# Gathering tokens for 32 experts with one fp32 copy and an unsplit fp32 bias in place of three bf16 parts

## The chip, the cores and the metric

The kernel runs on one core of a Trainium2 chip. The metric is device time in microseconds (us): the median of several executions. TensorE is called PE in the rows, and its weight loads PEld; DVE is VectorE, ACT is ScalarE, POOL is GpSimd, SP is SyncE, whose queue issues the loads of weights.

## What is computed

Two transformer blocks of two and one layers on 256 tokens of width 1024, all in fp32. The first block (an RG-LRU mixer, a forgetting attention, two squared-ReLU MLPs) and the hybrid mixer of the second block (stick-breaking attention beside an HGRN2 recurrence) are not touched by the change. What follows them is:

```python
h = layer_norm(ALPHA * h + mix, ln1_g, ln1_b)
ffn = moe(h, router_w, router_b, w_up, b_up, w_down, b_down)
h = layer_norm(ALPHA * h + ffn, ln2_g, ln2_b)

def moe(h, ...):
    logits = xt @ router_w + router_b            # 256 x 32
    top_vals, top_idx = lax.top_k(logits, 4)
    gates = jax.nn.softmax(top_vals, axis=-1)
    ...
    hcat = xblk @ w_up[e] + b_up[e]              # 1024 -> 2048
    x_glu = jnp.minimum(hcat[:, 0::2], 7.0)
    x_lin = jnp.clip(hcat[:, 1::2], -7.0, 7.0)
    act = x_glu * jax.nn.sigmoid(1.702 * x_glu) * (x_lin + 1.0)
    return act @ w_down[e] + b_down[e]           # 1024 -> 1024
```

Each of the 32 experts computes the block for the tokens that chose it, and each token sums its four experts' rows by its gates.

## The kernel before

*Dense part.* Up to about 830 us the kernel runs the two mixers, the MLPs and the projections. A weight arrives as a raw fp32 block of 1 MiB, `[128, 2048]`, is split into a rounded high part and a low rest (`split_to`, L370: ScalarE casts, VectorE or GpSimd subtracts), and `three` (L468) multiplies with three matmuls. The raw blocks rotate over a pool `rawA` of `NA = 5`, and `load_ahead` (L347) issues them on SP's queue.

*Experts.* After the router, `expert(pos)` (L1984) runs 32 times, in an order that `rank_experts` finds from the counts: position 0 and 1 hold experts 0 and 1, whose weights are known beforehand, and the rest are sorted. A unit is 64 slots for tokens. Every position has one unit, but position 12 has two (`WIDE`), so there are 33 units. For each, in this order on PE:

- `first_bias` (L1542): four matmuls that spread the expert's row of `b_up` over the 64 slots. `bup3` holds the 32 rows of `b_up` three times, as three bf16 parts, on 96 partitions; the weights are a 0/1 column of `Qb` that picks the three rows.
- `first_layer` (L1745): 8 chunks of `w_up`, each 1 MiB, four fp32 matmuls of 512 columns to a chunk, with the 64 gathered tokens as weights. Both halves of the output lie in two banks, a lower and an upper 64 partitions each. In the middle of it `combine` (L1835) adds the previous unit to the tokens.
- `turned_gates` (L1735): the tile `pG`, two transposes that give the slots' gates and the one-hot `PT`.
- `gather_units(pos + 1)` with `gather` (L1714): the next unit's tokens. The normed x is held in three bf16 parts `n3` whose sum is the fp32 value. For each of three parts, two token halves and eight feature blocks, one matmul has the part as weights (128 x 128) and the one-hot `P` (128 x 64) as moving operand: 48 matmuls into one bank `pX`. VectorE takes it out into `xT` with the norm's gain and bias.
- `turned` (L1790): the tile `paT`, the gated activation `xl` turned; and `second_layer` (L1801): four chunks of `w_down`.

While the first layer's results pass `gated` (L1758) on VectorE and ScalarE, PE does `pG` and the gather, which stand between the first layer and `paT` in its order.

```python
for i, t in ((0, 0), (1, 0), (0, 1), (1, 1), (2, 0), (2, 1)):
    for k in range(KT):
        pe.matmul(p[:, k], n3p[:, i, t, k // 2, k % 2], P[:, t],
```

*The order around it.* All order is that of the code. Small jobs that belong to expert 0 and 3 (ranking, `residual_sum`, `list_overflow`) are hung on chunks by the table `later` (L1974). The expert weights go through 20 chunk slots, 20 MiB. Some are filled by `fill` (L315) while the dense part still runs, as its pools close, and then `release` (L1987) calls `load_to`, which loads chunk n+20 when chunk n is used. A slot pool in `paired` holds two chunks that one DMA of 2 MiB loads; 12 of the 20 slots are such pairs. The other eight take 1 MiB each.

*Between router and experts.* The turned x for the router lies in `turned_x`, in one of the slots (`rawE`). The normed x is made in three parts by `high` (ScalarE, L1614) and `rest` (GpSimd for one token half, VectorE and ScalarE for the other, L1616 to L1632), interleaved with `best` and `chosen`, the routing. The bias parts are made earlier: `bias_parts` (L1459, VectorE casts) and `bias_rest` (L1463, GpSimd subtracts), hung among the last projections, whose weight splits (L368, L390) use the same engines. Before expert 0, PE also runs `pg`, eight transposes that spread the norm's gain over the tokens (L1682), for `residual_sum` (L1895).

Of the kernel before, what the change touches and what calls it, by code (L numbers as in the profile page):

```python
# [20 lines left out]
D = 1024  # L21
# [10 lines left out]
NA, NF, NG, NB = 5, 4, 2, 1  # L32
# [45 lines left out]
def shape_constants():  # L78
# [12 lines left out]
    f["ranks"] = np.broadcast_to(rank_of_position(), (128, NE))  # L91
# [6 lines left out]
    f["first"] = (i[:, None] % NE == np.arange(2)) & (i[:, None] < 3 * NE)  # L98
# [23 lines left out]
def fused(ctx: ExitStack, tc: tile.TileContext, d, out, dbg=None):  # L122
# [11 lines left out]
    rawA = ctx.enter_context(tc.tile_pool(name="rawA", bufs=NA, side="right"))  # L134

    def raw_tile():
        return rawA.tile([128, 2048], F32, tag="raw", name="raw")
# [209 lines left out]
    def load_ahead(n):  # L347
        while state["loaded"] < min(n, len(plan), *[i + NA for i in whole[:1]]):
            i = state["loaded"]
            r = raw_tile()  # L350
# [13 lines left out]
    def low_parts(left):  # L364

        while len(lows) > left:
            e, wl, src, wh = lows.pop(0)
            e.tensor_sub(wl, src, wh)  # L368

    def split_to(h):  # L370

        while state["split"] <= min(h, 2 * len(plan) - 1):
# [12 lines left out]
            for q in (slice(0, 512), slice(512, 1024)) if i == 0 else (slice(0, 1024),):  # L385
                copy, sub = [e[n % len(e)] for e in state["share"]]
                if copy == "d":
                    dve.tensor_copy(wh[:, q], src[:, q])
                else:
                    act.copy(wh[:, q], src[:, q])  # L390
                lows.append((pool if sub == "p" else dve, wl[:, q], src[:, q], wh[:, q].bitcast(F32)))
            low_parts(1 if state["late"] else 0)
            k, c = plan[i][1], 2048 // plan[i][1]
# [785 lines left out]
    with ExitStack() as mixo, ExitStack() as attn:  # L1179
# [239 lines left out]
        fill((4, second), (6, rawA), (7, rawA))  # L1419
# [5 lines left out]
        third = ctx.enter_context(tc.tile_pool(name="third", bufs=1, side="right", reuse_waits="tile"))  # L1425
        fill((10, third))
# [18 lines left out]
        rawB = ctx.enter_context(tc.tile_pool(name="rawB", bufs=NB, side="right", reuse_waits="tile"))  # L1445
        bup = rawB.tile([128, 2048], F32, tag="raw", name="bup")
        for g in range(3):
            sp.dma_start(bup[32 * g:32 * g + 32], d["expert_b_up_2"][0])
# [4 lines left out]
        mb = ctx.enter_context(tc.tile_pool(name="bias", bufs=1, side="right", reuse_waits="tile"))  # L1453
        bup3 = mb.tile([128, 2 * D], BF, name="bup3")
        pool.memset(bup3[96:128], 0.0)

        def bias_parts(n):

            dve.tensor_copy(bup3[:n], bup[:n])  # L1459

        def bias_rest(n):
            for c in (0, 1024):
# [4 lines left out]
        branch(1, 1, "w_branch_hgrn_2", [lambda: (bias_parts(96), bias_rest(64))])  # L1467
# [5 lines left out]
        first_b = mo.tile([128, 2], BF, name="first_b")  # L1473
# [4 lines left out]
        pool.tensor_copy(first_b, C("first"))  # L1478
# [35 lines left out]
        def out_proj(w, steps, first=False, hooks={}):  # L1514
            for i, k in steps:
# [4 lines left out]
                for f in hooks.get(i, ()):  # L1520
                    f()

        out_proj(w, [(i, i) for i in range(4)], True, {1: [lambda: bias_parts(64), lambda: bias_rest(32)]})
        w = row_weights(d["w_out_2"][0], 512, 512)
        out_proj(w, [(0, 4), (1, 5)], False, {0: [lambda: bias_parts(32)]})
# [24 lines left out]
        xs = [turned_x[:, t].rearrange("p (k t) -> p k t", k=KT) for t in range(2)]  # L1550
        n3 = mo.tile([128, 3, 2, D], BF, name="n3")
# [56 lines left out]
        def halves(t, c):  # L1608
            return x[:, t, c * 512:(c + 1) * 512], parts_of[:, t, c * 512:(c + 1) * 512], \
                [n3[:, i, t, c * 512:(c + 1) * 512] for i in range(3)]  # L1610

        def high(t, c):
            xx, rr, nn = halves(t, c)
            act.activation(nn[0], xx, AF.Identity, scale=rn[t], bias=nm[t])  # L1614

        def rest(t, c):  # L1616

            xx, rr, nn = halves(t, c)
            if t == 0:
                pool.tensor_scalar(rr, xx, rn[t], nm[t], op0=OP.mult, op1=OP.add)  # L1620
                yield
                pool.tensor_sub(rr, rr, nn[0])
                act.copy(nn[1], rr)
                yield
                pool.tensor_sub(nn[2], rr, nn[1])
            else:
                dve.scalar_tensor_tensor(rr, xx, rn[t], nn[0], op0=OP.mult, op1=OP.subtract)
                yield
                act.activation(nn[1], rr, AF.Identity, bias=nm[t])
                yield  # L1630
                dve.scalar_tensor_tensor(nn[2], rr, nm[t], nn[1], op0=OP.add, op1=OP.subtract)
            yield  # L1632

# [527 lines left out]
```

## Time and profile before

| what | value |
|---|---|
| median of 3 runs | 1775.71 us (1775.11 to 1777.3) |
| the profiled execution, its time | 1776.4 us |
| the profiled execution, its span | 1774.6 us |
| mean granted clock of TensorE | 0.983 |
| busy share: PE, PEld, DVE, ACT, POOL | 94%, 63%, 52%, 29%, 5% |
| mean DMA rate over the span, bytes moved | 303 GB/s, 538.55 MB |
| first layer of expert 0 begins | 839.11 us |
| last expert begins | 1725.88 us |

The span runs from the first to the last instruction; the execution's time is 1.8 us longer. A busy share is an average over a dense part and an expert part, which have different limits. In the timeline, adjacent instructions of one line are one row: "x32" counts the matmul records, of which an fp32 matmul has two, and the time of a row reaches to the end of the last, while the next row may begin before, since matmuls are pipelined. The time from start to start is what a group of them costs. A granted clock of 1.00 is 2.4 GHz, the lower level is 1.2 GHz.

### The profile page before, as it was taken

The numbers are of one execution on the slowest core, as the hardware profiler recorded it, in microseconds if no ns is written. First come the engines' busy times: TensorE is split into PE (matmuls) and PEld (weight loads), VectorE is DVE, ScalarE is ACT, GpSimd is POOL, SyncE is SP. The second block draws the span as 40 slices with busy tenths as digits, with TensorE's granted clock in tenths as the row PEclk, the third lists the DMA queues.
The fourth block names the chain that finished last, engine by engine and source line by source line (L and its number), as shares of the span: only waits on it lengthen the run. The fifth ranks groups of instructions, "written<-read, shape, count | busy, mean of one in ns | idle before, by whom it ended". The sixth has DMA issues, their size and how long they took to land.

```text
span 1774.6 us, 28179 instructions
## 1 busy us (share of the span) xinstructions
PE 1665.0 (94%) x11633; PEld 1112.0 (63%) x11633; DVE 928.4 (52%) x1681; ACT 514.4 (29%) x793; POOL 91.1 (5%) x102
## 2 busy tenths in 40 slices
PE   8999999989999999999998999999999988898895
PEld 8899998988999999997333333343333333333331
DVE  7776668677665667777435334334334333333233
ACT  5654444545444455544110010101010110101011
POOL 4020000001000001125000000000000000000000
PEclk9999999999999999999999999999999999999998
DMA  8465554333555544477999999999999999999995
GB/s 276 145 220 186 190 181 140 109 124 126 180 188 190 173 161 143 169 285 277 406 425 423 425 424 422 425 424 423 422 424 424 424 425 422 425 423 424 423 424 217
DMA packets 102532, 538.55 MB, mean 303 GB/s; under 512 B 7985, under 2 KB 21457, under 8 KB 68001
## 3 DMA queue, kind: packets, MB, share of 16 engines
q1 hardware_dynamic: 101520, 534.69, 76.7%
q0 software_dynamic: 736, 1.95, 0.4%
q8 instruction: 93, 1.52, 0.4%
q14 instruction: 39, 0.31, 0.0%
q10 hardware_dynamic: 144, 0.07, 0.0%
HBM read 535.64 MB, written 1.05 MB: 302 GB/s over the span
## 4 chain that ended last, share of the span: by engine, by line
PE 61%; DMA 21%; DVE 10%; ACT 4%; issue 2%; POOL 1%; SPq 0%; ACTq 0%; DVEq 0%; POOLq 0%
DMA raw<-in_expert_w_up_dram 21%; PE hp L1754 15%; PE py L1818 8%; PE pf L471 5%; PE pf L469 5%; PE pf L470 5%; PE a L470 4%; PE a L471 4%; PE a L469 4%; DVE wl L368 2%; PE a L826 1%; PE pC L1840 1%; DVE xl L1778 1%; DVE sgm L1775 1%; PE paT L1796 1%
## 5 line engine op out<-in xcount | busy, mean ns | idle before, releaser
L1754 PE MATMUL hp<-raw,xT 128*64 128x512 f32 x2112 | 479.1, 605 | 25.3 <-DMA raw<-in_expert_w_up_dram 24.5
L368 DVE TENSOR_TENSOR wl<-raw,wh 128x1024 fp32r<-128x1024 f32 (+1 forms) x235 | 288.2, 1244 | 140.8 <-ACT wh L390 138.7
L1754 PEld LDWEIGHTS hp<-raw,xT 128*64 128x64 f32 x2112 | 150.4, 139 | 316.7 <-issue 264.5
L390 ACT CAST wh<-raw 128x1024 fp32r<-128x1024 f32 (+1 forms) x238 | 242.1, 1039 | 170.4 <-PE pf L470 94.5
L471 PE MATMUL pf<-hH,wl 128*128 128x256 f32 x928 | 259.8, 280 | 7.4 <-DVE wl L368 7.4
L469 PE MATMUL pf<-hH,wh 128*128 128x256 f32 x928 | 261.9, 282 | 1.1 <-ACT wh L390 1.0
L470 PE MATMUL pf<-hL,wh 128*128 128x256 f32 x928 | 258.9, 279 | 0.0
L1818 PE MATMUL py<-raw,aT 128*64 128x512 f32 x1056 | 236.0, 599 | 17.4 <-ACT aT L1798 16.4
L471 PEld LDWEIGHTS pf<-hH,wl 128*128 128x128 f32 x928 | 174.3, 188 | 9.3 <-DVE wl L368 9.3
L469 PEld LDWEIGHTS pf<-hH,wh 128*128 128x128 f32 x928 | 174.3, 188 | 1.8 <-ACT wh L390 1.5
L1831 DVE SCALAR_TENSOR_TENSOR y<-py,gcol,y 64x512 fp32r<-64x512 f32 x66 | 49.5, 751 | 238.1 <-ACT y L1830 238.0
L470 PEld LDWEIGHTS pf<-hL,wh 128*128 128x128 f32 x928 | 174.0, 187 | 0.1
L1818 PEld LDWEIGHTS py<-raw,aT 128*64 128x64 f32 x1056 | 73.1, 137 | 158.0 <-issue 131.2
L1841 DVE TENSOR_TENSOR x<-x,pC 128x512 f32<-128x512 f32 x128 | 79.4, 682 | 176.6 <-PE pC L1840 176.6
L1769 ACT ACTIVATE sgm<-sgm 128x256 f32<-128x256 f32 x66 | 27.5, 417 | 492.2 <-DVE sgm L1768 492.2
L471 PE MATMUL a<-aH,wl 128*128 128x256 f32 x512 | 145.0, 283 | 0.0
L469 PE MATMUL a<-aH,wh 128*128 128x256 f32 x512 | 144.9, 283 | 0.0
L470 PE MATMUL a<-aL,wh 128*128 128x256 f32 x512 | 144.9, 283 | 0.0
L1830 ACT ACTIVATE y<-py,gcol 64x512 fp32r<-64x512 f32 x66 | 45.1, 683 | 261.2 <-issue 219.9
L1768 DVE TENSOR_SCALAR sgm<-hp 128x256 f32<-128x256 f32 x66 | 27.7, 419 | 145.0 <-PE hp L1754 145.0
L469 PEld LDWEIGHTS a<-aH,wh 128*128 128x128 f32 x512 | 98.3, 192 | 0.0
L471 PEld LDWEIGHTS a<-aH,wl 128*128 128x128 f32 x512 | 98.2, 192 | 0.0
(494 smaller groups left out, 2082.7 us busy)
## 6 DMA issues: line engine op xcount, KB each, us to landing
raw<-in_expert_w_up_dram SPq DMA_DIRECT2D x77, 2048.0 KB, 24.8
raw<-in_expert_w_up_dram SPq DMA_DIRECT2D x102, 1024.0 KB, 24.7
raw<-in_expert_w_down_dram SPq DMA_DIRECT2D x38, 2048.0 KB, 24.8
raw<-in_mlp_w_dram SPq DMA_DIRECT2D x64, 1024.0 KB, 5.4
raw<-in_expert_w_down_dram SPq DMA_DIRECT2D x51, 1024.0 KB, 24.8
raw<-in_w_in_dram SPq DMA_DIRECT2D x22, 1024.0 KB, 5.2
raw<-in_fox_w_in_dram SPq DMA_DIRECT2D x12, 1024.0 KB, 5.4
raw<-in_lru_w_in_dram SPq DMA_DIRECT2D x6, 1024.0 KB, 12.9
```

The lines of the kernel that those rows point to most:

```text
L368: e.tensor_sub(wl, src, wh)
L390: act.copy(wh[:, q], src[:, q])
L469: pe.matmul(out_ap, lh, rh, start=first, stop=False, skip_group_check=True)
L470: pe.matmul(out_ap, lh, rl, start=False, stop=False, skip_group_check=True)
L471: pe.matmul(out_ap, ll, rh, start=False, stop=last, skip_group_check=True)
L1754: pe.matmul(hp[b][64 * g:64 * g + 64], xT[:, k], w[:, c0:c0 + 512], start=False, stop=(k == KT - 1), skip_group_check=True)
L1768: dve.tensor_scalar_min(sgm[b], hv[b][:, :, 0], 7.0)
L1769: act.activation(sgm[b], sgm[b], AF.Sigmoid, scale=1.702)
L1818: pe.matmul(py[c], aT[:, j, g * 64:(g + 1) * 64], w[:, i * D + c * 512:i * D + c * 512 + 512], start=(kt == 0), stop=(kt == KT - 1), skip_ ...
L1830: act.activation(y[0:64, s], py[c], AF.Copy, scale=gcol[h])
L1831: dve.scalar_tensor_tensor(y[64:128, s], py[c], gcol[h], y[0:64, s].bitcast(F32), op0=OP.mult, op1=OP.subtract)
L1841: dve.tensor_add(x[:, t, s], x[:, t, s], p)
```

## The change

1. The normed x becomes one fp32 tile `nx` that four ScalarE operations write. The turned x for the router lies in the same tile before. `high`, `rest`, `parts_of` and `n3` are gone, and GpSimd's part in them.
2. `gather` has 16 fp32 matmuls (eight blocks, two token halves) in place of 48 in bf16; `P` is fp32. In expert 0 it writes three banks in turn, otherwise one, taken out by two VectorE operations of 128x512 in place of four of 128x256.
3. `bup` holds the bias unsplit: each quarter of 512 columns on 32 partitions of its own. `Q` has four blocks of 0/1 columns, and `first_bias` four fp32 matmuls. `bias_parts` and `bias_rest` are gone.
4. `rawA` is one tile `area`, of which parts serve as raw blocks and as slots. 18 of 20 slots are in pairs. The last four dense loads rotate over three blocks of it. Slot pair 18 takes the place that `turned_x` had, at the closing of `wp2x`, and the third pair of slots (10) is filled later, after the attention's pools close.
5. In expert 0, `residual_sum` and its `pg` matmuls are at chunk 5, `by_position` at chunk 4, and the bias of expert 1 at chunk 7. Some memsets are smaller or gone.

```diff
-        for g in range(3):
-            sp.dma_start(bup[32 * g:32 * g + 32], d["expert_b_up_2"][0])
+        bup = mb.tile([128, 512], F32, name="bup")
+        for g in range(4):
+            sp.dma_start(bup[32 * g:32 * g + 32], d["expert_b_up_2"][0][:, g * 512:(g + 1) * 512])
...
-            dve.tensor_copy(bup3[:n], bup[:n])
...
-                pool.tensor_sub(bup[:n, c:c + 1024], bup[:n, c:c + 1024], bup3[:n, c:c + 1024])
...
+            k = (i - TAKEN) % NA if i < TAKEN else 2 + (i - TAKEN) % 3
+            r = area[:, k * 2048:(k + 1) * 2048]
...
-        fill((4, second), (6, rawA), (7, rawA))
+        fill((4, second), (6, parts_A[0]))
...
-        turned_x = rawE.tile([128, 4, D], F32, tag="raw", name="turned_x")
+        fill((18, rawE))
...
-        fill((11, rawA), (12, rawA), (13, rawA))
+        fill((12, parts_A[1]), (16, parts_A[2]))
...
         def first_bias(hps, sel):
...
-                        c0 = g * D + b * 512
-                        pe.matmul(hp[b][64 * g:64 * g + 64], sel.to_broadcast([128, SLOTS]),
-                                  bup3[:, c0:c0 + 512], start=True, stop=False, skip_group_check=True)
+                        pe.matmul(hp[b][64 * g:64 * g + 64], sel[:, 2 * g + b].to_broadcast([128, SLOTS]), bup,
+                                  start=True, stop=False, skip_group_check=True)
...
-        n3 = mo.tile([128, 3, 2, D], BF, name="n3")
+        nx = mo.tile([128, 2, D], F32, name="nx")
+        xs = [nx[:, t].rearrange("p (k t) -> p k t", k=KT) for t in range(2)]
...
-        for t, c in ((1, 0), (0, 0), (1, 1), (0, 1)):
-            high(t, c)
+        for t in range(2):
+            for c in range(2):
+                h = slice(c * 512, (c + 1) * 512)
+                act.activation(nx[:, t, h], x[:, t, h], AF.Identity, scale=rn[t], bias=nm[t])
...
-        for i, t in ((0, 0), (1, 0), (0, 1), (1, 1), (2, 0), (2, 1)):
-            for k in range(KT):
-                pe.matmul(p[:, k], n3p[:, i, t, k // 2, k % 2], P[:, t],
-                          start=(i + k + t == 0), stop=(i == 2 and t == 1), skip_group_check=True)
+        for s in (slice(0, 2), slice(2, 5), slice(5, 8)) if quick else (slice(0, KT),):
+            p = mm("pX").rearrange("p (k s) -> p k s", k=KT)
+            for k in range(s.start, s.stop):
+                for t in range(2):
+                    pe.matmul(p[:, k], nxp[:, t, k // 2, k % 2], P[:, t], start=(k == s.start and t == 0),
+                              stop=(k == s.stop - 1 and t == 1), skip_group_check=True)
...
-        dve.tensor_scalar(Q, C("ranks"), rk, None, op0=OP.is_equal)
-        dve.tensor_copy(Qb, Q)
+        dve.scalar_tensor_tensor(rk4, rk.to_broadcast([128, 4]), 1.0, C("block"), op0=OP.add, op1=OP.mult)
+        dve.tensor_tensor(Q, C("ranks")[:, None, :].to_broadcast([128, 4, NE]),
+                          rk4[:, :, None].to_broadcast([128, 4, NE]), op=OP.is_equal)
...
-        (0, 1): [lambda: residual_sum(1), gates_of_tokens],
+        (0, 1): [gates_of_tokens],
...
-        (0, 5): [by_position],
+        (0, 4): [by_position],
+        (0, 5): [residual_sum],
+        (0, 7): [lambda: first_bias(early_hps[1], first_b[:, :, 1:2])],
```

The order of instructions on PE around the start of the experts, before. `cd`, `pl` are the router's operands, `route_b` the constants that count tokens before each one; of rows that repeat a pattern the first stand here:

```order
L1581 MATMUL pl<-cd,turned_x 128x32 x8
L1547 LDWEIGHTS first_b
L1547 MATMUL hp<-bup_8541,first_b 64x512
...
L1682 MATMUL pg<-ident,V 128x128 x8
L1685 LDWEIGHTS route_b
L1685 MATMUL prk<-M_8823,route_b 128x32
...
L1720 LDWEIGHTS n_8820
L1720 MATMUL pX<-P_8992,n_8820 128x64
```

And in the changed kernel:

```order
L1587 MATMUL pl<-cd,nx 128x32 x8
L1552 MATMUL hp<-bup,cf 64x512 x4
L1654 LDWEIGHTS route_b
L1654 MATMUL prk<-M_8683,route_b 128x32
...
L1685 MATMUL pX<-P_8830,nx 128x64 x16
L1719 MATMUL hp<-raw,xT 64x512 x4
```

The `pg` matmuls and the bias of expert 1 no longer stand between the router and the gather, and bias and gather, now fp32, have no rows for weight loads of their own.

One expert of the middle on PE, before:

```order
L1754 MATMUL hp<-raw,xT 64x512 x16
L1739 MATMUL pG<-ident,G 128x128 x2
L1720 LDWEIGHTS n_8820
L1720 MATMUL pX<-P,n_8820 128x64
...
L1796 MATMUL paT<-ident,xl 128x128 x4
L1818 MATMUL py<-raw,aT 64x512 x16
L1547 LDWEIGHTS Qb
L1547 MATMUL hp<-bup_8541,Qb 64x512
```

And in the changed kernel:

```order
L1719 MATMUL hp<-raw,xT 64x512 x16
L1704 MATMUL pG<-ident,G 128x128 x2
L1685 MATMUL pX<-P,nx 128x64 x16
L1761 MATMUL paT<-ident,xl 128x128 x4
L1783 MATMUL py<-raw,aT 64x512 x16
L1552 MATMUL hp<-bup,Q 64x512 x4
```

The places are the same; the gather is still between `pG` and `paT`, and the next bias still behind the second layer.

## Rows read from the trace of the kernel before

**Rows 1.** The page, the span in 40 equal slices: DMA rate of each.
```profile
GB/s 276 145 220 186 190 181 140 109 124 126 180 188 190 173 161 143 169 285 277 406 425 423 425 424 422 425 424 423 422 424 424 424 425 422 425 423 424 423 424 217
```

**Rows 2.** Stretches: us, busy us by engine, granted clock, DMA share, GB/s.
```profile
820.00:829.00 9.00, 9.00 (x63) 7.87 (x61) 5.42 (x30) 4.46 (x8) 0.00 (x0) 1.00 0.24 67
...
921.77:954.39 32.62, 26.88 (x165) 11.25 (x163) 17.66 (x34) 2.85 (x6) 0.00 (x0) 0.95 1.02 427
954.39:1164.30 209.91, 201.61 (x1315) 80.43 (x1313) 79.26 (x189) 22.77 (x48) 0.00 (x0) 1.00 1.01 423
...
1218.84:1402.00 183.16, 175.33 (x1107) 69.18 (x1108) 69.16 (x164) 19.92 (x42) 0.00 (x0) 1.00 1.01 424
1402.00:1725.88 323.88, 288.66 (x1740) 110.94 (x1738) 106.63 (x253) 31.30 (x66) 0.00 (x0) 0.97 1.01 424
```

**Rows 3.** Timeline of TensorE, one expert of the middle: start, us, operation, count, idle.
```profile
1059.07 0.60 PE L1547 MATMUL hp<-bup,Qb 128*64 128x512 bf16 x4
1059.50 7.04 PE L1754 MATMUL hp<-raw,xT 128*64 128x512 f32 x32
1066.47 1.20 PE L1840 MATMUL pC<-y,PT 128*128 128x512 f32 x4
...
1074.89 1.56 PE L1720 MATMUL pX<-P,n 128*128 128x64 bf16 x48
1077.11 0.74 PE L1796 MATMUL paT<-ident,xl 128*128 128x128 f32 x4 [0.66 <-DVE xl L1778]
```

**Rows 4.** Waits on TensorE, 1402 to 1725.88: us in total, times, longest.
```profile
PE hp L1754 <- DMA raw<-in_expert_w_up_dram: 22.0, 11, 3.2
```

**Rows 5.** Timeline of TensorE, the last expert: its two gaps for weights.
```profile
1733.00 3.65 PE L1754 MATMUL hp<-raw,xT 128*64 128x512 f32 x16 [1.84 <-DMA raw<-in_expert_w_up_dram]
...
1742.87 3.65 PE L1754 MATMUL hp<-raw,xT 128*64 128x512 f32 x16 [0.72 <-DMA raw<-in_expert_w_up_dram]
```

**Rows 6.** Timeline of TensorE: fp32 matmuls of 128 weight columns, and what follows.
```profile
815.41 3.73 PE L1535 MATMUL a<-cd,x 128*128 128x128 f32 x32
818.90 0.48 PE L469 MATMUL a<-wh,mH 128*128 128x512 f32 x1
819.21 0.39 PE L470 MATMUL a<-wl,mH 128*128 128x512 f32 x1
819.44 0.40 PE L471 MATMUL a<-wh,mL 128*128 128x512 f32 x1
...
826.07 1.87 PE L1581 MATMUL pl<-cd,turned_x 128*128 128x32 f32 x16
827.78 0.63 PE L1576 MATMUL pT<-ident,x 128*128 128x128 f32 x4
```

**Rows 7.** Timeline of TensorE: before and at the start of the experts.
```profile
806.81 0.49 PE L469 MATMUL a<-wh,mH 128*128 128x512 f32 x1 [0.64 <-ACT wh L390]
808.39 0.50 PE L470 MATMUL a<-wl,mH 128*128 128x512 f32 x1 [1.09 <-DVE wl L368]
...
809.66 0.62 PE L469 MATMUL a<-wh,mH 128*128 128x512 f32 x1
...
813.06 0.41 PE L471 MATMUL a<-wh,mL 128*128 128x512 f32 x1
...
831.08 3.22 PE L1682 MATMUL pg<-ident,V 128*128 128x128 f32 x16
...
835.74 0.51 PE L1720 MATMUL pX<-P,n 128*128 128x64 bf16 x12 [0.61 <-DVE P L1605]
...
839.11 1.94 PE L1754 MATMUL hp<-raw,xT 128*64 128x512 f32 x8 [0.50 <-ACT xT L1724]
```

**Rows 8.** Timeline of VectorE: parts of the normed x among the routing.
```profile
830.01 1.22 DVE L1627 SCALAR_TENSOR_TENSOR parts_of<-x,l1q,n 128x512 f32<-128x512 f32 x1 [0.25 <-ACT n L1614]
...
834.22 1.01 DVE L1627 SCALAR_TENSOR_TENSOR parts_of<-x,l1q,n 128x512 f32<-128x512 f32 x1
```

More of the change, by code (lines that the diff above doesn't have):

```diff
@@ L133, in fused, with __init__, tile @@
     ps = ctx.enter_context(tc.tile_pool(name="ps", bufs=4, space=PSUM))
-    rawA = ctx.enter_context(tc.tile_pool(name="rawA", bufs=NA, side="right"))
-    def raw_tile():
-        return rawA.tile([128, 2048], F32, tag="raw", name="raw")
+    rawA = ctx.enter_context(tc.tile_pool(name="rawA", bufs=1, side="right"))
+    area = rawA.tile([128, NA * 2048], F32, name="area")
+    class Part:
+        def __init__(self, k, n):
+            self.ap = area[:, k * 2048:(k + n) * 2048]
+        def tile(self, shape, dtype, tag=None, name=None):
+            assert shape == [128, self.ap.shape[1]] and dtype == F32
+            return self.ap
+    parts_A = [Part(0, 2), Part(3, 2), Part(2, 1)]
+    singles_A = [Part(k, 1) for k in range(4)]
     def mm(name="mm"):
@@ L1452, in fused @@
         sp.dma_start(rbr, d["router_b_2"].to_broadcast([128, NE]))
[L1453 to L1457, printed above, removed]
-            dve.tensor_copy(bup3[:n], bup[:n])
-        def bias_rest(n):
-            for c in (0, 1024):
-                pool.tensor_sub(bup[:n, c:c + 1024], bup[:n, c:c + 1024], bup3[:n, c:c + 1024])
         branch(1, 0, "w_branch_hgrn_2")
         state["share"] = ("a", "d")
-        branch(1, 1, "w_branch_hgrn_2", [lambda: (bias_parts(96), bias_rest(64))])
+        branch(1, 1, "w_branch_hgrn_2")
         mixo.close()
@@ L1606, in spread @@
                               rc.to_broadcast([128, 2, SLOTS]), op=OP.is_equal)
[L1608 to L1632, printed above, removed]
         pls = {}
@@ L1649, in fused @@
         paired.append(rawC)
-        fill((14, rawC), (16, rawB))
+        rawF = ctx.enter_context(tc.tile_pool(name="rawF", bufs=1, side="right", reuse_waits="tile"))
+        fill((14, rawC), (17, rawF))
         pls[0], pls[1] = mm("pl"), mm("pl")
@@ L1678, in fused @@
         early_hps = [[[bank("hp") for _ in range(2)]] for _ in range(2)]
-        first_bias(early_hps[0], first_b[:, 0:1])
-        gain = [mm("pg") for _ in range(2)]
-        for k in range(KT):
-            pe.matmul(gain[k // 4][:, k % 4 * 128:k % 4 * 128 + 128], vc("ln1_g", k).to_broadcast([128, 128]), ident,
-                      start=(k % 4 == 0), stop=True, skip_group_check=True)
+        first_bias(early_hps[0], first_b[:, :, 0:1])
         pr = mm("prk").rearrange("p (a e) -> p a e", e=NE)
@@ L1696, in fused @@
     dense.close()
-    rawF = ctx.enter_context(tc.tile_pool(name="rawF", bufs=1, side="right", reuse_waits="tile"))
-    fill((17, rawF), (18, rawE))
-    slots = [first] * 4 + [second] * 2 + [rawA] * 2 + [rawD] * 2 + [third] + [rawA] * 3 + [rawC] * 2 + \
-        [rawB, rawF] + [rawE] * 2
+    slots = [first] * 4 + [second] * 2 + [parts_A[0]] * 2 + [rawD] * 2 + [third] * 2 + [parts_A[1]] * 2 + \
+        [rawC] * 2 + [parts_A[2], rawF] + [rawE] * 2
     stream["next"] = len(slots)
@@ L1893, in gates_of_tokens, with residual_sum @@
             dve.tensor_scalar_mul(RG[:, 1, t], lg[:, t], gs[:, t:t + 1])
-    def residual_sum(c):
-        s = slice(c * 512, (c + 1) * 512)
-        for t in range(2):
-            act.activation(x[:, t, s], x[:, t, s], AF.Identity, scale=rn[t], bias=nm[t])
-            dve.scalar_tensor_tensor(x[:, t, s], x[:, t, s], ALPHA, gain[c], op0=OP.mult, op1=OP.mult)
+    def residual_sum():
+        for c in range(2):
+            s = slice(c * 512, (c + 1) * 512)
+            gain = mm("pg")
+            for k in range(4):
+                pe.matmul(gain[:, k * 128:(k + 1) * 128], vc("ln1_g", 4 * c + k).to_broadcast([128, 128]), ident,
+                          start=(k == 0), stop=True, skip_group_check=True)
+            for t in range(2):
+                dve.scalar_tensor_tensor(x[:, t, s], nx[:, t, s], ALPHA, gain, op0=OP.mult, op1=OP.mult)
     def start_sum(c):
@@ L1906, in start_sum @@
             p = mm("pbd")
-            pe.matmul(p, RGT[:, 1, t * 128:(t + 1) * 128], rows[:, s], start=True, stop=True)
+            pe.matmul(p, RGT[:33, 1, t * 128:(t + 1) * 128], rows[:33, s], start=True, stop=True)
             dve.tensor_add(x[:, t, s], x[:, t, s], p)
```

99 lines of the change are left out of this document (42 added, 57 removed).

## The prediction, made before the changed kernel ran

> **What bounds the kernel now.** I read the 40 slices first [rows 1]. Up to about 830 us the weights come at 109 to 285 GB/s, then 406 in one slice; from there to the end the rate stands at 422 to 425 GB/s, so the expert stage is the one place where a transfer can be the limit. Whether it is has to be read expert by expert. Cutting the stage at the starts of experts [rows 2] gives three regimes. The eight experts from 954.39 take 209.91 us, 26.24 each; the seven from 1218.84 take 183.16 us, 26.17 each; the eleven from 1402.00 take 323.88 us, 29.44 each. One expert is twelve MiB of weights, 12.58 MB, and at 424 GB/s that is 29.7 us. So the kernel starts the stage with 20 MiB in its slots and eats that lead at 26.17 us an expert, which is TensorE's own pace, and when the lead is gone, near 1430 us, it falls back to the pace of the stream.
>
> The TensorE timeline of one expert of the middle regime [rows 3] shows that nothing but TensorE sets its 26.17 us: bias, first layer, gates, gather, turn and second layer follow each other, with one gap of 0.66 us at the turn `paT`, where VectorE's product `xl` is late. This gap matters: the gather stands right before it. The gather starts at 1074.89 and `paT` cannot start before 1077.11, so the gather has 2.22 us of time that is free, and uses about 1.4 to 1.56 of it.
>
> In the late regime the waits on the queue of TensorE [rows 4] name the weights: 22.0 us on first-layer chunks. By intervals the loss is 323.88 - 11 x 26.17 = 36.0 us, since a late chunk is followed by smaller gaps that no row names. The last expert waits another 1.84 + 0.72 = 2.6 us [rows 5]. So **38.6 us of slack** is all that more work on TensorE can hide in; beyond that every microsecond that the change adds to TensorE comes out at the end.
>
> **The change, part by part.** All but a few instructions keep their order, so I cost it as a sum on TensorE.
>
> *Bias.* Four bf16 matmuls of 512 columns become four fp32 ones of the same output shape, once per unit of 64 slots (33 units: 32 experts, one of them twice as wide). The bf16 ones take 0.43 us from start to the next start (1059.07 to 1059.50). An fp32 matmul with 64 weight columns and 512 moving ones is the first-layer matmul itself: 32 records, two to a matmul, in 6.97 us (1059.50 to 1066.47 in its whole run; the row gives 7.04 with the drain) [rows 3], 0.218 us a record. Eight records are 1.74 us, so +1.31 us a unit. Nothing covers it: the first layer follows in order, into the same banks. Unit 0's bias lies before the stage; expert 1's moves into expert 0 and counts whole, 1.74; the other 31 give 40.6 us.
>
> *Gather.* 48 bf16 matmuls become 16 fp32 ones, of 128 weight columns and 64 moving. No row has this shape. The nearest has 128 moving columns: 32 records from 815.41 to the next operation at 818.90, 3.49 us, 0.109 a record [rows 6]. The router's matmuls have only 32 moving columns and cost the same, 16 records from 826.07 to 827.78, 0.107 each. A price that does not change between 32 and 128 columns is that of the weights, and holds for 64 between them. I take 32 x 0.109 = 3.5 us. Against the 2.22 us that are free, +1.28 us an expert; the other way, counting all of it beyond today's 1.41 us, +2.1. The lower end is nothing at all, should it fit into the 2.22; the upper end doubles the price per record, +4.8 an expert. 29 gathers at 1.28 give 37.1. Position 11 gathers two units in one window, +4.2; position 12, in which the other unit follows, has no free window, +2.1; expert 3, whose gates are late and whose clock is low for a while (0.95 on average over its stretch) [rows 2], gets +0.6. Together 44.0 us.
>
> The Trainium skill, FP8 and Floating Point Precision, section TensorE Precision Notes, says that true FP32 takes four passes through the array. Counted by passes alone, the gather would be 16 x 4 x 64 columns, at 2.4 GHz an estimate of 1.71 us, which would fit into the free window; by it the time would be some 1779 us in place of 1821. The two rows that cost the same at 32 and 128 columns speak against it; it is the first rival below.
>
> *Moved into expert 0.* The eight `pg` matmuls (16 records at 0.109) go from before the stage into expert 0: +1.75.
>
> *The waits for weights.* They go, 38.6 us, if TensorE becomes slow enough. The new pace is 26.17 + 1.31 + 1.28 = 28.8 us an expert. That is still 0.9 us less than the stream's 29.7, but over the 19 experts behind the wide one that eats 17 us of a lead of 20 chunks of 2.47 us, 49 us, and the additions ahead of it (some 40 us) have by then filled all slots. So the stream never binds again, and earlier and larger loads buy nothing in this stage.
>
> *Before the stage.* First-layer work begins at 839.11 [rows 7]. The casts and subtractions of the bias are gone; they delayed the weight splits for `w_out`, so TensorE waited 0.64 and 1.09 us, and then ran eight matmuls at 1.2 GHz, 809.66 to 813.06, 0.43 each in place of the 0.23 that such a one has at 2.4 GHz (819.21 to 819.44) [rows 6]: 1.6 more. Of these 3.3 us I count 3. VectorE loses two operations of 1.22 and 1.01 us out of the chain from router logits to one-hot [rows 8]; the `pg` block of 3.2 us [rows 7] leaves TensorE's queue; the gather no longer waits for three kinds of parts. Against this stand the fp32 bias (+0.7 to +1.3) and an fp32 gather in place of a bf16 one whose 3.37 us with its waits (835.74 to 839.11) it roughly equals. I take -4.5 in all, between -10 (3.3 at the splits, 2.2 in the routing, 3.2 of `pg` and the waits of the gather, 0.61 and 0.50, all gained) and 0. The dense loads ahead of it now rotate over three blocks at the end instead of five, and the pairs of slots stand elsewhere on SP's queue; at 67 GB/s between 820 and 829 us [rows 2], the queue has room, so nothing, with one landing of about 5 us as the other end. On VectorE two operations of 512 columns replace four of 256, which is no more work; ScalarE and GpSimd only lose work, and are idle there.
>
> **Sum**, against the profiled execution, whose span is 1774.6 and whose time is 1776.4: -4.5 - 38.6 + 40.6 + 1.7 + 1.8 + 44.0 = +45.0, a span of 1819.6. With the 1.8 us outside the span 1821.4; the profiled execution lies 0.7 above the median, so **1821 us**.
>
> **Rivals.**
> 1. *The gather fits into its window.* For it: it has a third as many matmuls and no split operands. At 2.2 us a gather only position 11 (4.4 - 2.8 = +1.6) and position 12 (+0.8) pay, 2.4 in place of 44.0, and the time is 1821 - 42 = 1779. Against it the rows of 32 and 128 columns. Chance 0.06.
> 2. *The stream stays the bound and is quicker: faster than before.* Place: the late regime. It decides if bias and gather together add under about 1 us a unit, for example when the bias too runs beside other work; then TensorE is never the limit after 1430 us. The slots are full earlier (the 9 us at 67 GB/s before 829 are worth up to 7 us of streaming; I count 4), and 18 of 20 slots go in 2 MiB transfers; the highest rate in the windows, 427 against 424 GB/s, over 900 us gives 6. Time 1776 - 10 = 1766. Against it: the bias is priced by a row of its own shape, and alone takes 40.6 of the 38.6. Chance 0.04.
> 3. *The clock falls after each gather.* The gather stretch has few moving columns per microsecond. The trace has the clock low after gaps: 809.66 to 813.06 follows two waits, and it cost 1.6 us. At every one of 32 experts that is +51, 1872; at half of them 1846. Against it: the stretch of 32 fp32 records at 815.41 is followed by matmuls at 0.31 and then 0.23 spacing, full speed. Chance 0.08, mostly for part of the experts.
> 4. *Each record costs double*, say because weights and moving columns do not overlap with changing weights: +3.5 x 32 = 112, 1933. Chance 0.02.
>
> That the change does not do what it says is excluded by the order of its instructions: the gather and bias rows carry no separate weight load and have the new counts.
>
> **How the numbers follow.** A measurement of this kernel tells about 0.2%, 3.5 us, from no change. The forecast has 0.80. Its own range is 1809 to 1833: the hand-over between -10 and 0, 0.2 us either way on each gather. The range of 8 in 10 reaches down to 1806, for a gather 0.3 us cheaper, and up to 1846, half of the experts with a low clock; it leaves out rivals 1, 2, 4 and a part of 3. Faster by over 0.2%: rival 2 and the lower tail of 1, 0.05. Within: most of rival 1, 0.04. Slower: 0.91.
>
> **What would show it.** Right: gather stretches of about 3.5 us; bias of 1.74; no gap at `paT`; the waits for weights on TensorE gone from the late regime and experts there at 28.8 us, the same as in the middle; DMA rate under 424 GB/s in the middle, as SP waits for slots; first layer at about 834.6. Wrong: if the gap at `paT` is still there, the gather was hidden; if late experts still stand at 29.4 or more with waits for weights, the stream binds; if the middle experts take over 30 us, look at the clock.

## The result

The changed kernel takes 1831.16 us (median; 1830.61 to 1836.11) against 1775.72 us before: a ratio of 1.0317, with an interval of 1.0298 to 1.0336. It is slower by 55 us; the forecast was 1821 us, 45 us slower, in a range of 1806 to 1846.

The page of the changed kernel, 40 slices. The first row is the granted clock in tenths, the last the DMA rate, which answers to [rows 1]:

```profile
PEclk9999999999999999999989999999999999999998
...
GB/s 268 137 236 185 185 185 121 134 93 158 185 185 187 189 159 134 258 289 294 396 390 378 427 424 427 426 353 244 417 424 427 427 426 426 425 426 426 426 422 49
```

The last slice is the first thing to see: it moves 49 GB/s. Before, the stream ran into the last expert; now it is done earlier, and it has pauses in between (353 and 244), where it waits for TensorE to give slots back. In the slices of 417 to 427 GB/s it is not held up: one expert is 12.58 MB, so at 28.88 us an expert TensorE asks for 436 GB/s and lives on its lead there too, only more slowly than before.

The expert stage cut at the starts of experts, which answers to [rows 2] (us, busy us by engine, granted clock, DMA share, GB/s):

```profile
831.73:898.36 66.63, 65.71 (x323) 28.64 (x324) 23.73 (x61) 6.72 (x14) 0.00 (x0) 0.95 0.80 324
898.36:927.24 28.88, 28.42 (x149) 12.44 (x147) 9.55 (x21) 2.85 (x6) 0.00 (x0) 1.00 1.01 423
927.24:966.87 39.63, 34.14 (x153) 16.23 (x151) 17.51 (x32) 2.85 (x6) 0.00 (x0) 0.83 0.80 331
966.87:1169.03 202.16, 198.93 (x1024) 86.97 (x1022) 66.88 (x147) 19.93 (x42) 0.00 (x0) 1.00 1.01 426
...
1201.68:1262.22 60.54, 56.51 (x262) 22.80 (x258) 16.30 (x37) 5.69 (x12) 0.00 (x0) 0.94 0.61 234
...
1464.43:1782.11 317.68, 312.60 (x1608) 136.75 (x1606) 105.06 (x231) 31.32 (x66) 0.00 (x0) 1.00 1.01 425
```

The seven experts from 966.87 take 28.88 us each, and so do the eleven from 1464.43: the two regimes of before, 26.17 and 29.44, have become one, at TensorE's new pace. The row of 60.54 us is position 12, with its two units: there the stream pauses. One expert of the common pace on TensorE, which answers to [rows 3]:

```profile
1053.51 1.89 PE L1552 MATMUL hp<-bup,Q 128*64 128x512 f32 x8
1055.23 3.60 PE L1719 MATMUL hp<-raw,xT 128*64 128x512 f32 x16
...
1070.61 3.88 PE L1685 MATMUL pX<-P,nx 128*128 128x64 f32 x32
1074.33 0.68 PE L1761 MATMUL paT<-ident,xl 128*128 128x128 f32 x4
```

The bias takes 1.72 us from start to start, where it took 0.43; the gather 3.72, where 2.22 were free. The gap before `paT` is gone. All waits of TensorE from 840 us to the end, which answer to [rows 4]:

```profile
PE py L1783 <- ACT aT L1763: 16.4, 32, 2.1
PE pG L1704 <- DVE G L1697: 6.2, 2, 5.0
PE fin L2030 <- DVE y L1796: 1.6, 1, 1.6
PE paT L1761 <- DVE xl L1743: 1.2, 1, 1.2
PE pC L1805 <- DVE x L1806: 0.3, 1, 0.3
```

None of them is for weights. The hand-over to the experts, which answers to [rows 7]:

```profile
823.23 1.94 PE L1552 MATMUL hp<-bup,cf 128*64 128x512 f32 x8
...
826.43 5.37 PE L1685 MATMUL pX<-P,nx 128*128 128x64 f32 x32 [0.73 <-DVE M L1660]
831.73 3.68 PE L1719 MATMUL hp<-raw,xT 128*64 128x512 f32 x8
```

The first layer begins at 831.73, 7.4 us earlier than before, although the gather ahead of it ran partly at 1.2 GHz (5.30 us to the next start, against 3.72 elsewhere), and the first layer began at it too (3.68 us for eight records that took 1.94 in [rows 7]). Not all of the 7.4 us belong to the change. 2.1 us of them are there at 670 us already, in the first block, whose computing the change does not touch: the profiled execution of the kernel before had TensorE at 1.2 GHz there for longer. In the profiles of the kernels with the change the same point comes at 664.8 to 670.5 us, in the kernel before at 669.4. In the rest, the end of the weight splits gives 4.7 us and the routing 2.0, and the fp32 gather takes 1.5 back.

Laid beside the forecast, stretch by stretch, all from starts in the two traces:

| stretch | forecast | measured |
|---|---|---|
| before the first layer of expert 0 | -4.5 | -7.4 |
| experts 0 and 1 | +6.1 | +10.1 |
| expert 2 | +2.6 | +2.7 |
| expert 3 | +3.2 | +7.0 |
| positions 4 to 10 | +18.1 | +19.0 |
| positions 11 and 12 | +10.2 | +11.9 |
| positions 13 to 30 | +10.6 | +12.9 |
| last expert | -1.3 | -1.9 |
| sum (spans 1774.6 and 1829.0) | +45.0 | +54.4 |

### The profile page after: what moved, and what is told of

Its sections match the earlier page's. It is cut to its first block, busy times and chain, and to the rows that moved or that the text cites. A ratio compares the mean times of both kernels' runs of the same rounds, so it can differ in the third digit from the quotient of the medians.

```text
span 1829.0 us, 27058 instructions
## 1 busy us (share of the span) xinstructions
PE 1768.7 (97%) x11237; PEld 1197.0 (65%) x11237; DVE 911.6 (50%) x1610; ACT 509.7 (28%) x785; POOL 67.7 (4%) x87
## 4 chain that ended last, share of the span: by engine, by line
PE 89%; DVE 6%; ACT 3%; issue 1%; POOL 1%; DMA 0%; SPq 0%; ACTq 0%; DVEq 0%; POOLq 0%
PE hp L1719 25%; PE py L1783 13%; PE pX L1685 7%; PE pf L487 5%; PE pf L489 5%; PE pf L488 5%; PE a L489 4%; PE a L487 4%; PE a L488 4%; PE hp L1552 3%; PE pC L1805 2%; DVE wl L385 1%; PE a L844 1%; PE paT L1761 1%; PE pS L1066 1%
## 5 line engine op out<-in xcount | busy, mean ns | idle before, releaser
L385 DVE TENSOR_TENSOR wl<-area,wh 128x1024 fp32r<-128x1024 f32 (+1 forms) x235 | 285.3, 1232 | 141.7 <-ACT wh L407 139.9
L1719 PE MATMUL hp<-raw,xT 128*64 128x512 f32 x1576 | 352.7, 596 | 0.0
L407 ACT CAST wh<-area 128x1024 fp32r<-128x1024 f32 (+1 forms) x238 | 242.3, 1039 | 173.1 <-PE pf L488 94.3
L1719 PEld LDWEIGHTS hp<-raw,xT 128*64 128x64 f32 x1576 | 111.0, 137 | 219.0 <-issue 215.6
L1783 PE MATMUL py<-raw,aT 128*64 128x512 f32 x800 | 179.9, 599 | 8.8 <-ACT aT L1763 8.8
L1685 PE MATMUL pX<-P,nx 128*128 128x64 f32 x1056 | 133.8, 288 | 0.7 <-DVE M L1660 0.7
L1685 PEld LDWEIGHTS pX<-P,nx 128*128 128x128 f32 x1056 | 132.6, 204 | 0.8 <-issue 0.8
L1783 PEld LDWEIGHTS py<-raw,aT 128*64 128x64 f32 x800 | 55.9, 138 | 117.6 <-issue 102.5
L1719 PE MATMUL hp<-area,xT 128*64 128x512 f32 x536 | 124.1, 602 | 0.0
```

Of the source, the lines that this page charges most:

```text
L1685: pe.matmul(p[:, k], nxp[:, t, k // 2, k % 2], P[:, t], start=(k == s.start and t == 0), stop=(k == s.stop - 1 and t == 1), skip_group_che ...
L1719: pe.matmul(hp[b][64 * g:64 * g + 64], xT[:, k], w[:, c0:c0 + 512], start=False, stop=(k == KT - 1), skip_group_check=True)
L1783: pe.matmul(py[c], aT[:, j, g * 64:(g + 1) * 64], w[:, i * D + c * 512:i * D + c * 512 + 512], start=(kt == 0), stop=(kt == KT - 1), skip_ ...
```

## The experiments

Theory A is that of the prediction: every matmul that the change adds to TensorE comes out at the end, once the 38.6 us of slack are used. Theory B puts the loss on the loads: the new blocks, pairs and slots. A third question is what sets the price of an fp32 gather.

### The bias alone back in bf16 parts

```diff
-        sel = Q[:, :, pos:pos + 1] if pos > 1 else None
+        sel = (Q[:, :, pos:pos + 1] if pos < 4 else Qb[:, pos:pos + 1]) if pos > 1 else None
...
+            for n in (96, 64, 32):
+                pool.tensor_copy(bup3[:n, c:c + 1024], b_raw[:n])
+                if n > 32:
+                    pool.tensor_sub(b_raw[:n - 32], b_raw[:n - 32], bup3[:n - 32, c:c + 1024])
```

> The changed kernel, but from position 4 on the bias is again three bf16 parts stacked on 96 partitions (four bf16 matmuls a unit), made by GpSimd during the first experts in the block of one slot; 18 slots in place of 20. Theory A (TensorE sets the pace and every matmul added to it comes out at the end): the 29 units concerned save 1.72 - 0.43 = 1.29 us each, 37 us, so 1794 us, with experts of the middle at 27.6 us and no waits for weights, or few at the very end. Theory B (the loss is in the loads: blocks, pairs and slots rearranged, the expert stage waiting for SP's queue): nothing changes, 1831 us or more, since there are two slots fewer.

Measured: 1804.68 us, ratio to the kernel before 1.0164 (1.0146 to 1.0182), 26 us less than the changed kernel. The experts of the middle take 27.59 us, 28.88 - 1.29, to the hundredth as forecast; their bias and gather:

```profile
1055.09 0.60 PE L1694 MATMUL hp<-area,Qb 128*64 128x512 bf16 x4
1055.52 3.60 PE L1744 MATMUL hp<-area,xT 128*64 128x512 f32 x16
...
1070.90 3.88 PE L1710 MATMUL pX<-P,nx 128*128 128x64 f32 x32
```

The time is 11 us above theory A's 1794. In experts 27 to 30 the intervals are 28.1 to 30.0 us, and TensorE waits 4.7 us for weights: at 27.59, and with 18 slots, the lead runs out shortly before the end, and 6.7 us of the gain are given back. Expert 2 begins 4.9 us later than in the changed kernel: the stage starts 3.0 us later, and expert 1 has more of its time at the lower clock. Theory B falls: with two slots fewer the kernel is faster.

### The gather alone back in bf16 parts

```diff
+            if pos > 2:
+                gather_parts(ready[no]["P"], ready[no]["xT"])
+            else:
+                gather(ready[no]["P"], ready[no]["xT"], pos == 0)
...
+        (1, 0): [part_one],
+        (2, 0): [rest_one],
+        (2, 1): [part_two],
+        (2, 4): [part_three],
```

> The changed kernel, but the gathers of position 3 and later are again 48 bf16 matmuls over three parts, which ScalarE and VectorE make out of the fp32 tile in experts 1 and 2; the bias stays fp32; 18 slots in place of 20. Theory A: the 26 plain gathers save 28.88 - 26.17 - 1.29 = 1.42 us each, expert 3 about 4 (its gather ran at the lower clock, 7.0 against 2.8 us), positions 11 and 12 about 5 and 2: 48 us, so 1783 us, experts at 27.5 us, the gap of 0.66 us before the turn back. Theory B: 1831 us.

Measured: 1789.51 us, ratio 1.0084 (1.0067 to 1.0101), 42 us less than the changed kernel. The experts of the middle take 27.45 us, and the gap before the turn is back:

```profile
1060.64 1.56 PE L1711 MATMUL pX<-Pb,n 128*128 128x64 bf16 x48
1062.86 0.75 PE L1784 MATMUL paT<-ident,xl 128*128 128x128 f32 x4 [0.66 <-DVE xl L1766]
```

Experts 26 to 30 stand at 28.3 to 29.7 us, with 6.0 us of waits for weights, 9 us above 27.45 in all; that is more than the 6 us by which the time is above theory A's 1783.

### Both back, with the change's loads

The two edits together.

> Both together, bias and gather in bf16 parts again from position 4 and 3 on, with the early loads and the pairs of the changed kernel, 18 slots. Theory A alone would add the two savings: 1831 - 37 - 48 = 1746 us. But then the stream becomes the bound again: 364 to 366 MiB behind the first 18 to 20 at 424 to 427 GB/s from about 835 us, and some 30 us of last expert behind the last chunk: 1760 to 1770 us, so the savings do not add, experts of the second half stand at 29.5 us with waits for weights, those of the middle at 26.2. If larger and earlier loads are worth nothing, 1776 us as before the change. Theory B: 1831 us.

Measured: 1782.27 us, ratio 1.0038 (1.0027 to 1.005). The savings of 26 and 42 us do not add to 68: 49 remain. From position 21 on the experts stand at 29.2 to 30.3 us, and TensorE waits 26.9 us for first-layer weights, as in [rows 4]:

```profile
PE hp L1768 <- DMA raw<-in_expert_w_up_dram: 17.9, 17, 2.0
...
PE hp L1768 <- DMA area<-in_expert_w_up_dram: 9.0, 9, 1.3
```

The form is that of theory A, but the floor is not at 1760 to 1770: it is above the kernel before. Where the stream lost is read from its rate in early stretches of this kernel:

```profile
829.00:840.00 11.00, 11.00 (x52) 5.96 (x52) 4.39 (x12) 1.99 (x3) 8.46 (x9) 0.69 0.16 50
840.00:860.00 20.00, 19.71 (x119) 10.60 (x116) 10.72 (x26) 3.23 (x6) 7.83 (x8) 1.00 1.01 372
860.00:880.00 20.00, 19.54 (x75) 6.33 (x74) 7.28 (x8) 3.91 (x5) 3.80 (x3) 0.91 0.81 306
...
1500.00:1700.00 200.00, 174.15 (x1072) 66.72 (x1072) 64.76 (x145) 18.57 (x40) 0.00 (x0) 0.99 1.01 427
```

and the same stretches of the kernel before:

```profile
829.00:840.00 11.00, 8.88 (x90) 6.53 (x91) 10.35 (x23) 8.08 (x15) 8.69 (x9) 0.84 0.99 395
840.00:860.00 20.00, 18.85 (x138) 7.93 (x136) 10.11 (x37) 5.91 (x11) 2.09 (x5) 1.00 0.97 398
860.00:880.00 20.00, 20.00 (x84) 6.96 (x82) 6.96 (x13) 1.36 (x2) 0.00 (x0) 1.00 1.01 412
...
1500.00:1700.00 200.00, 177.64 (x1080) 68.92 (x1080) 66.49 (x160) 19.24 (x41) 0.00 (x0) 0.97 1.01 424
```

The earlier loads are done before 829 us; then all slots are full, and the stream stands nearly still until expert 0 gives slots back: a share of 0.16 where the kernel before has 0.99. Between 860 and 880 it slows down again, to 306 GB/s. What SP's queue waited for between 815 and 900 us (us in total, times, longest):

```profile
SPq L324 <- PE hp L1768: 43.3, 6, 18.3
```

It waits for first-layer matmuls to be done with their slots, once for 18.3 us; the longest such wait of the kernel before is 7.9 us. What was loaded early is so repaid with idle time, and the rate of 427 in place of 424 GB/s does not make up for it. This kernel has 18 slots, two fewer than the kernel before: 2 MiB, or 4.9 us of the stream. How much of the loss is theirs was not separated; the mixture below has all 20, and its stream pauses too.

### Half of the gather's columns

```diff
-                    pe.matmul(p[:, k], nxp[:, t, k // 2, k % 2], P[:, t], start=(k == s.start and t == 0),
+                    pe.matmul(p[:, k, :32], nxp[:, t, k // 2, k % 2], P[:, t, :32], start=(k == s.start and t == 0),
```

> The changed kernel, with only 32 of the 64 one-hot columns streamed through each of the 16 gather matmuls; the result of the first 32 slots is written to the other 32 as well, so half of the tokens' slots are left out. Prices by weights (the theory of the prediction): 32 records at 0.11 us are unchanged, the gather takes 3.6 to 3.7 us from start to the turn, 1831 us. Prices by moving columns (the rival): the gather halves to 1.9 us, fits into the 2.2 us that are free, and the time falls by 1.4 us on each of 32 experts, to about 1785 us.

Measured: 1875.19 us, ratio 1.0565 (1.0532 to 1.0598): half the columns cost 44 us more. One gather and what follows:

```profile
1166.65 3.85 PE L1685 MATMUL pX<-P,nx 128*128 128x32 f32 x32
1170.34 0.71 PE L1763 MATMUL paT<-ident,xl 128*128 128x128 f32 x4
1171.51 2.44 PE L1785 MATMUL py<-raw,aT 128*64 128x512 f32 x6 [0.46 <-ACT aT L1765]
```

The gather takes 3.69 us with 32 columns and 3.72 with 64: its price is not that of the columns. That it is that of the weight loads, and not a fixed price of an fp32 record, is seen in the rows of the loads, six gathers of this kernel (count, busy us, mean ns, idle us before), and in a small matmul of the changed kernel:

```profile
L1685 PEld LDWEIGHTS pX<-P,nx 128*128 128x128 f32 x192 | 23.1, 196 | 0.0
...
940.64 0.27 PE L1890 MATMUL pcp<-Q,cnt 32*1 32x32 f32 x4
940.84 3.65 PE L1719 MATMUL hp<-raw,xT 128*64 128x512 f32 x16
```

The loads fill the gather without idle time, 3.85 us for each 32. The four records of `pcp`, also fp32 with 32 moving columns but with one weight column (on 32 rows; the token sums below show no price of rows), take 0.05 us each, where those with 128 weight columns take 0.107 in [rows 6] and 0.115 here. The Trainium skill, FP8 and Floating Point Precision, section TensorE Precision Notes, has four passes for true FP32; counted in columns that would be an estimate of 0.85 us for this gather, where 3.69 are measured. With 512 columns the trace comes near it: the four matmuls of the token sums, shown further down, take 3.63 us, by four passes 3.41. The 44 us come from elsewhere, which neither theory had: six records of the second layer take 2.44 us, where 16 take 3.6 at 2.4 GHz. In 19 of the 31 intervals from one `pG` to the next the expert takes 30.2 to 30.6 us in place of 28.88, at a mean granted clock of 0.95: after the gather the clock falls to 1.2 GHz for a while, though TensorE waits no longer there than in the changed kernel. In five intervals it does not fall, and why in some and not in others was not found. That is rival 3 of the prediction, and it needed half as many columns to come true.

### The operands of the gather exchanged

```diff
+        for t in range(2):
+            for c in range(2):
+                pe.matmul(p[64 * c:64 * c + 64], P[:, t], nx[:, t, c * 512:(c + 1) * 512],
+                          start=(t == 0), stop=(t == 1), skip_group_check=True)
...
+        act.copy(r.rearrange("a (m j p) -> a m j p", m=2, j=2), p.rearrange("a (m p j) -> a m j p", m=2, j=2))
...
+        for q in range(4):
+            pe.transpose(p[:, q * 128:(q + 1) * 128], r[:, q * 128:(q + 1) * 128], ident)
```

> The changed kernel, all of it in fp32, but with the operands of the gather exchanged for positions 2 and later (not 13): the one-hot is the weight operand (64 columns) and the normed x the moving one, four matmuls of 512 columns, then ScalarE copies the 64 slots out and four transposes in the middle of the second layer turn them. If the price is that of the weight loads: 1.74 us as for the bias, inside the 2.2 us that are free, and 0.5 us for the transposes, so 28.88 - 1.42 + 0.5 = 28.0 us an expert, some 25 to 32 us in all: 1799 to 1806 us. If fp32 itself is the price, whatever the operands: 28.9 us and 1831 or more, for the transposes.

Measured: 1804.91 us, ratio 1.017 (1.0151 to 1.0188), 26 us less than the changed kernel with every operand still fp32. One expert takes 28.19 us:

```profile
1088.44 1.94 PE L1700 MATMUL pX<-nx,P 128*64 128x512 f32 x8
1090.57 0.75 PE L1794 MATMUL paT<-ident,xl 128*128 128x128 f32 x4 [0.19 <-DVE xl L1776]
...
1093.65 0.66 PE L1716 MATMUL pX<-ident,xrows 128*128 128x128 f32 x4
```

Eight weight loads of 64 columns in place of 32 of 128, and the gather fits between `pG` and the turn. The four transposes add 0.6 us. So fp32 is not dear as such; its weight loads are. The 26 us are not all of this kind: 0.69 us on each expert of the common pace, and 4.5 us in expert 3 (35.13 us in place of 39.63), whose gather takes 3.50 us.

### The list of overflowing experts later, in both kernels

```diff
-        (3, 5): [list_overflow],
+        (3, 8): [list_overflow],
```

On the changed kernel:

> The changed kernel with one edit: the list of overflowing experts, 8.4 us of VectorE work in expert 3, hangs on chunk 8 in place of chunk 5, behind the gates instead of ahead of them. Theory A: expert 3 takes 39.63 us where others take 28.88; 5.03 of that is the wait for the gates, the rest the fp32 gather and the second layer at the lower clock that follows the wait. Where TensorE is the bound all of it is on the path, so 10 to 11 us go: 1820 to 1822 us, and expert 3 at about 29. If the wait only moves, to the gated activation or to the slots' sums, less than 3 us go.

Measured: 1819.52 us, ratio 1.0234 (1.0218 to 1.0249), 12 us less. Expert 3 takes 29.2 us, from 932.09 to 961.32. In the changed kernel it was the expert with the wait, and with the clock behind it:

```profile
949.52 0.69 PE L1704 MATMUL pG<-ident,G 128*128 128x128 f32 x2 [5.03 <-DVE G L1697]
950.00 7.00 PE L1685 MATMUL pX<-P,nx 128*128 128x64 f32 x32
956.79 1.06 PE L1761 MATMUL paT<-ident,xl 128*128 128x128 f32 x4
```

The gather takes 6.79 us there, nearly all of it at 1.2 GHz; with the list moved it takes 3.72. The kernel with the gather in bf16 parts has the same wait of 5.0 us, but a granted clock of 0.95 over expert 3, as before the change, where the changed kernel has 0.83: the clock fell in all three, and was at 1.2 GHz for longer only where the fp32 gather followed.

On the kernel before:

> The kernel before the change, with the one edit that gained 11 us on the changed kernel: the list of overflowing experts hangs on chunk 8 of expert 3 in place of chunk 5. Expert 3 should take 26.2 us in place of 32.62, so TensorE is 6 us further at position 4. If the kernel before is bound by the stream over the whole expert stage (its rate is 423 to 424 GB/s from 840 us on), the 6 us come back as waits for weights in the last ten experts and the time stays within 0.2%: 1776 us. If TensorE's time counts there too, 1769 to 1770 us.

Measured: 1774.77 us, ratio 1.0003 (0.9992 to 1.0014). Expert 3 takes 26.5 us in place of 32.62, and the waits for first-layer weights grow from 24.5 us to this:

```profile
PE hp L1754 <- DMA raw<-in_expert_w_up_dram: 30.5, 19, 3.0
```

One edit, 6 us of TensorE's time in the one kernel and 10 in the other (with the fp32 gather at the lower clock): nothing where the stream is the bound, all of it where TensorE is.

### Transfers of 1 MiB in place of 2

```diff
+        if two and len(parts) == 1:
+            ap = parts[0][1]
+            n = ap.shape[1] // 2
+            parts = [(0, ap[:, :n]), (2048, ap[:, n:])]
```

> The kernel with bias and gather back in bf16 parts, which is bound by the stream, with each load of 2 MiB for a pair of slots issued as two of 1 MiB, at the same place on SP's queue. If the size of the transfers makes the 427 GB/s of that kernel out of the 424 GB/s before the change: 0.7% of some 900 us, 1788 us. If the size is worth nothing: 1782 us.

Measured: 1792.42 us, ratio 1.0088 (1.0073 to 1.0104), 10 us more than the same kernel with 2 MiB. Its rate late in the stage, 419 GB/s against 427:

```profile
1500.00:1700.00 200.00, 175.03 (x1024) 61.06 (x1020) 61.35 (x135) 18.46 (x38) 0.00 (x0) 1.00 1.01 419
```

So the pairs are worth 10 us where the stream is the bound. In the changed kernel TensorE is the bound, and they are worth nothing to be seen.

### The fastest mixture

The exchanged gather, the later list, and the bias in bf16 parts (kept behind the dense part's memory, split in eight pieces), with all 20 slots.

> The exchanged gather, the later list and the bias in bf16 parts from position 4 on, with all 20 slots and the pairs and early loads of the change. TensorE's pace is 26.2 + 0.5 = 26.7 us an expert, under the stream's 29.5, so the stream is the bound. It is ahead of the kernel before up to 860 us, some 1 MiB behind at 950 for the slower experts 0 and 1, and gains 0.7% by its rate: 1768 to 1775 us. If the two changes of the hand-over and the pairs were worth what they are meant for, 1766; if the slots are short again in experts 0 to 3, 1780.

Measured: 1780.04 us, ratio 1.0023 (1.0013 to 1.0034). It is 51 us under the changed kernel and does not beat the kernel before. Its pace is 26.9 us an expert, and only experts 26 to 30 stand at 29.2 to 30.7. The stream slows down at the hand-over here too: 159 GB/s from 829 to 840 us and 253 from 860 to 870, for want of free slots. A version that beats both was not found. One with the kernel before's arithmetic and timing of loads, and more of its slots in pairs, was not tried.

### The token sums with 128 rows again

```diff
-            pe.matmul(p, RGT[:33, 1, t * 128:(t + 1) * 128], rows[:33, s], start=True, stop=True)
+            pe.matmul(p, RGT[:, 1, t * 128:(t + 1) * 128], rows[:, s], start=True, stop=True)
```

> The changed kernel, with the four matmuls that begin the token sums (at the end of expert 0) fed with 128 rows again, 95 of them zeros, in place of 33 rows. The matmuls take the same 3.70 us. In the changed kernel the 16 records that follow them run at 1.2 GHz in part (5.34 us in place of 3.6), in the kernel before they do not. If the 33 rows bring the clock down, expert 1 starts its upper half 1.7 us earlier and the stretch behind the token sums is at 2.4 GHz: 1829 us. If the clock falls for another reason (its phase, the bias of expert 1 ahead), the low stretch is still there: 1831 us.

Measured: 1829.07 us (1824.74 to 1834.99), ratio 1.0302 (1.0287 to 1.0318): as a time not to be told from the changed kernel. In the trace the place is clear. The changed kernel:

```profile
865.83 3.70 PE L1878 MATMUL pbd<-rows,RGT 33*128 33x512 f32 x8
869.46 5.34 PE L1719 MATMUL hp<-area,xT 128*64 128x512 f32 x16
```

and with 128 rows:

```profile
870.80 3.70 PE L1878 MATMUL pbd<-rows,RGT 128*128 128x512 f32 x8
874.43 3.65 PE L1719 MATMUL hp<-area,xT 128*64 128x512 f32 x16
```

The sums take 3.70 us either way. Behind the 33 rows the next 16 records take 5.34 us, behind 128 rows 3.65. The 1.7 us are there. That the 33 rows alone cause it is not shown: of the nine profiled kernels with 33 rows eight have the lower clock in this place, but the one with half of the gather's columns has not (3.65 us); none of the three with 128 rows has it. As for the time, other stretches at the lower clock, which fell differently in this execution (the first gather took 6.98 us from start to start in place of 5.30), hide them in the time.

## Why the prediction was right

**The bound.** Right: the slack of 38.6 us was all that TensorE's additions could hide in, the waits for weights are gone, and both regimes have become one pace, 28.88 us where 28.8 was forecast. The runs with one part undone show it from the other side, each by the lead that runs out when the pace falls under the stream's. One sign was wrong: the rate was to lie under 424 GB/s in the middle, as SP waits for slots. It was 426 there. The prediction's own figures say so, since 28.8 us an expert is less than the stream's 29.7; only at the hand-over, in expert 3 and at position 12 did full slots hold the stream up.

**The bias.** +1.29 us a unit against a forecast of +1.31; the row of the same shape was the right price.

**The gather.** +1.42 us an expert against +1.28. The step was right, its size 0.14 off: spaced 0.116 us a record, not 0.109, and 3.72 us to the turn, not 3.5. The reason, that weight loads and not columns set the price, was an inference from rows of 32 and 128 columns; the run with half the columns, the row of `pcp` and the run with exchanged operands show it. Rival 1 falls with it.

**The hand-over.** -7.4 against -4.5, within its bounds of -10 and 0. 2.1 us of that is luck of the two executions, since it arose before 670 us. The change's own -5.3 is near the forecast, with a larger gain at the splits (4.7 in place of 3) and a dearer gather, partly at 1.2 GHz, which the prediction took as no dearer than the one in bf16.

**What was mis-sized.** Of the 9.4 us that the span moved beyond the sum, the hand-over gave 2.9 back, and the stretches lost 12.3. Experts 0 and 1 lost 4.1 of it, expert 3 3.8, positions 11 and 12 1.7, the rest 2.7. In expert 3 the step was the "+0.6" for an expert "whose clock is low for a while": the wait of 5.03 us was known, but a gather of 3.7 us at 2.4 GHz takes 6.8 at 1.2, and the second layer begins at it. In expert 0 the first layer's first eight records ran at 1.2 GHz (+1.7), and in expert 1 the stretch behind the 33-row sums (+1.7), an edit of the change that the prediction did not cost at all. The gather of position 12 too ran partly at 1.2 GHz, 4.96 us in place of 3.72. So the forecast of 45 us for a measured 55 had each part of the mechanism, and too little for the clock and for the gather.

**What was right for a weaker reason.** That "earlier and larger loads buy nothing in this stage" holds for the changed kernel, since TensorE is the bound. Rival 2 gave them 10 us where the stream is the bound. The run with both parts undone shows that the larger ones do give 10 us, by the split, and that nothing is left of the earlier ones: the slots are full at the hand-over, and the stream pauses until expert 0 gives them back. What in experts 0 and 1 keeps the slots busy longest was not taken apart.

## What to carry to other kernels

Before trading many cheap matmuls for few dear ones, price the weight loads in the new type, not matmuls or columns: an fp32 matmul whose 128 weight columns are used for 64 moving ones costs its two weight loads. The 48 bf16 matmuls of a gather took 1.4 us, 0.03 each; the 32 fp32 weight loads that replaced them took 0.116 each. Here it paid to make the operand with fewer columns the weights. Where a stream sets the end, ask how much slack the compute engine has over the whole run, and spend no more: the first 39 us here were free, each one after them cost full price. The same edit can be worth nothing in one kernel and 12 us in its successor, so a measured gain belongs to the bound under which it was measured.

## What was not expected of the hardware

- Fewer moving columns made a kernel slower: 32 in place of 64 left the gather at 3.69 us, and brought TensorE from 2.4 to 1.2 GHz for a stretch behind it in 19 of 31 intervals; the time rose by 44 us.
- Matmuls over 33 rows in place of 128 take the same time (3.70 us). In eight of nine kernels with 33 rows the ones behind them then ran at 1.2 GHz in part (5.34 us in place of 3.65 in the changed kernel), in none of three with 128 rows.
- Two transfers of 1 MiB in place of one of 2 MiB, back to back on one queue, lowered a saturated stream from 427 to 419 GB/s. The Trainium skill, DMA: Bandwidth & Descriptors, section Measured (HBM→SBUF, 128 partitions, SWDGE, issued from GpSimd), asks for at least 1 MiB per transfer, for at least 75% of the peak; here, issued from SP, twice that still gained 1.9% in rate.
